# A chunked DeltaNet mixer: decay tiles E in a ring of three, keys scaled on VectorE, z and o loaded into the memory of the gated output

## The chip, the cores and the metric

The kernel runs on one core of a Trainium2 chip. The metric is the time of one execution on the device in microseconds (us), lower is better. TensorE is written PE (PEld for its weight loads), VectorE DVE, ScalarE ACT, GpSimd POOL and the engine that issues most loads SP. Each engine takes its instructions strictly in the order of the program; where an instruction waits, all behind it on that engine wait too. A DMA that SP issues waits in the same way in SP's order.

## The reference

The model is two layers over 512 latent tokens and 256 context tokens of width 1024. The change lies almost wholly in the mixer of the second, odd layer, a bidirectional chunked gated DeltaNet with 8 heads of width 128:

```python
q, k, v, a, b, z = project(h)            # h @ w_in; k, q, v through a 7-tap convolution and silu
k = l2norm(k); q = l2norm(q) * Dh ** -0.5
for dirn in (0, 1):                      # forward and backward
    g, beta = gates(a, b, dirn)
    # per chunk: gcum = cumsum(g)
    decay = exp(where(lower, gcum_i - gcum_j, -inf))
    lmat  = where(strict, (beta k) k^T * decay, 0)
    u, w  = triangular_solve(lmat, [beta v, beta k exp(gcum)])
    aqk   = where(lower, q k^T * decay, 0)
    # scan over chunks: state S, output o from q, S, aqk and u - w S
o = o * rsqrt(mean(o * o) + eps) * norm_g
out = (o * silu(z)) @ w_out
```

After the mixer come a SwiGLU half and the final norm.

## The kernel before

The whole kernel is written as Python generators, one for each strand of work (`conv`, `norms`, `pre`, `subst`, `loop`, `place`, `levels`, `scan`, `finish`, and the main strand). A planner (`Flow`) runs them: it keeps a clock for each engine, prices each instruction (`account`), and always resumes the strand that could start first. The program's order on each engine is the order in which the planner resumed them; on the chip nothing of it is decided again. A changed price therefore can move any instruction of the program, in both layers.

In the odd mixer, called `mixer1`, the chunk is 128 tokens (6 chunks, 4 of latent tokens). The main strand runs the 24 projections of k, q and v and then the 8 of z on PE; each result is copied to a `pad` tile by ACT and convolved by DVE. For each head, in order:

- `norms` transposes k to `kn`, sums squares on ACT, takes a reciprocal root in nine small DVE steps (`rsq_r`), and multiplies `kn` by it. That multiplication is on POOL. PE then transposes `kn` back into `kT`.
- `pre` loads the cumulative gates of the head as `E` (one tile for each direction, 384 KB from the DRAM tensor `gd`, by SP), masks it with one `affine_select` on POOL, exponentiates it in six ACT instructions, and multiplies the products of PE by it on DVE: first `NT` (from k with k), then `aq` (from k with q). `EB = 1`: there is one tile for each direction, so the two loads for the next head are issued when both `aq` of this head are done.
- `subst` and `loop` solve the 32 x 32 triangles: 31 steps of two POOL instructions (`s5l<-lm,xm` and `xm<-xm,s5l`), 62 for each head. `place` and `levels` put the blocks together (`fX`, `fP`, `fQ`) on DVE, PE and ACT.
- `scan` runs the chunks of the two directions (`u`, `O`); `finish` normalises `O`, transposes it and stores it to DRAM (`ogd`).

The projections of z go to DRAM too (`zd`). After the last of them the memory of the mixer's input is free: the residual `xT` (2 MB) is loaded back, and the output pair `oT` (`oTh`, `oTl`, a high and a low part) is allocated. The strand `gated` takes the heads one after the other: it loads z and o of a head into two work tiles, multiplies on DVE, rounds to `oTh` on ACT and takes the rest to `oTl` on DVE. The output projection (`gout`) follows: 8 groups of 18 matmuls over heads 0 to 5, and a last part over heads 6 and 7.

All instructions are recorded at one line, L207 (L208 after), so groups are told apart by their tiles.

Of the kernel before, what the change touches and what calls it, by code (L numbers as in the profile page):

```python
# [10 lines left out]
F32 = mybir.dt.float32  # L11
# [3 lines left out]
AF = mybir.ActivationFunctionType  # L15
# [3 lines left out]
P = 128  # L19
# [42 lines left out]
EB = 1  # L62
# [6 lines left out]
MP = 5000.0  # L69
MPS = 9000.0  # L70
LAG = 1000.0
CU = 2
UNITS = {"ffn02": 3, "ffn11": 4, "ffn12": 6}
WCH = ((19, 20), tuple(range(9)), tuple(range(9, 16)), (16, 17, 18, 21))
# [4 lines left out]
class Flow:  # L79
# [51 lines left out]
    def account(self, eng, op, a, k):  # L131
        self.used = self.used or eng
        aps = [v for v in (*a, *k.values()) if isinstance(v, bass.AP)]
        outs = [aps[0]] + ([k["accum_out"]] if k.get("accum_out") is not None else [])
        ins = [v for v in aps[1:] if v is not k.get("accum_out")]
        t = max(self.free[eng], *(self.ready(v, eng) for v in aps))
        n = 1
        for s in aps[0].shape[1:]:
            n *= s
        if op == "dma_start":  # L140
            b = 4.0
            for s in aps[0].shape:
                b *= s
            if eng == "gpsimd":
                self.free[eng] = t + 1040.0
                t += 1040.0
            else:
                self.free[eng] = t + 60.0
                t += 1100.0
            self.dma = max(self.dma, t) + b / 360.0  # L150
            self.sent = self.dma + 900.0
            self.note(aps[0], self.sent, "dma")
            return
        banks = [self.bank_of[v.tensor.name] for v in aps if v.tensor.name in self.bank_of]
        if eng == "tensor":
            c = max(n / 2.4 * (1 if ins[-1].dtype == F32R else 2 if op == "transpose" else 4), 27.0)
        elif eng == "scalar":
            c = n / 1.2 + (51.0 if ins[0].tensor.name in self.bank_of else 93.0)
            c += 93.0 * (len(outs) > 1 or isinstance(k.get("scale"), bass.AP) or isinstance(k.get("bias"), bass.AP))
            s = self.TABLE.get(k.get("func", a[2] if len(a) > 2 else None))  # L160
            self.uset = self.uset or s
            if s and s != self.table:
                self.table = s
                c += 1283.0
        elif eng == "vector":
            m = 1
            for s in ins[0].shape[1:] if ins else ():
                m *= s
            two = op in ("tensor_tensor", "tensor_add", "tensor_sub", "tensor_mul", "tensor_max")
            c = max(n, m) / 0.96 + (69.0 if two or len(ins) < 2 else 130.0)  # L170
            if op == "scalar_tensor_tensor" and not isinstance(a[2] if len(a) > 2 else k.get("scalar"), bass.AP):
                c -= 61.0
            if op in ("tensor_scalar", "tensor_copy") and not banks:
                c -= n / 1.92
        else:
            c = n * 0.83 + 140.0 if op == "affine_select" else n / 1.2 + 60.0 if op == "memset" else n * 2.05 + 145.0
        t += c
        self.free[eng] = t
        for v in outs:
            self.note(v, t, eng)  # L180
        for b in banks:
            self.bank_used[b] = max(self.bank_used[b], t)
        if t > self.end:
            self.end, self.last = t, eng
# [101 lines left out]
class Kern:  # L286
# [1622 lines left out]
    def mixer1(self, ph, nxt):  # L1909
        nc, A, tc, flow = self.nc, self.A, self.tc, self.flow  # L1910
        V = nc.vector
# [101 lines left out]
        def ht(name, shape, bufs=1, dt=F32):  # L2013
            return hpool.tile(shape, dt, name=name, tag=name, bufs=bufs)
# [63 lines left out]
        def norms():  # L2078

            yield ("gates",)  # L2080
            for hd in range(8):
# [7 lines left out]
                kn = R["kn"] = ht("kn", [P, 6, P], 3)  # L2089
# [19 lines left out]
                yield  # L2109
                V.tensor_scalar(sq, sq, EPS, None, op0=ALU.add)  # L2110
                rs = yield from self.rsqrt(self.small, sq, [P, 10], "h")
                nc.gpsimd.tensor_mul(kn, kn, rs[:, :6][:, :, None].to_broadcast([P, 6, P]))
                sg = R["sg"] = ht("sg", [P, 4], 3)
                V.tensor_scalar(sg, rs[:, 6:10], float(P) ** -0.5, None, op0=ALU.mult)
                sG = R["sG"] = ht("sG", [P, 2, 4], 3)
# [12 lines left out]
        def pre():  # L2128

            yield ("gates",)  # L2130
            def load(hd):

                E = [ht(f"E{d}", [P, 6, P], EB) for d in range(2)]
                for d in range(2):
                    nc.sync.dma_start(E[d].rearrange("p c i -> p (c i)"),
                                      bass.AP(tensor=gd.tensor, offset=gd.offset + (8 * d + hd) * 6 * P,
                                              ap=[[96 * P, 4], [0, 32], [1, 6 * P]]))
                return E

            yield ("gd",)  # L2140
            E1 = load(0)
            for hd in range(8):
                R = H[hd]

                E = E1 if EB == 2 or hd == 0 else load(hd)
                if EB == 2 and hd < 7:
                    E1 = load(hd + 1)
                for d in range(2):
                    yield flow.landed(E[d])
                    nc.gpsimd.affine_select(out=E[d], in_=E[d], pattern=[[0, 6], [1 - 2 * d, P]], base=0,  # L2150
                                            channel_multiplier=2 * d - 1, compare_op=ALU.is_ge, fill=-1e30)
                    yield
                    for c in range(6):
                        nc.scalar.activation(E[d][:, c], E[d][:, c], AF.Exp, bias=nG[:, d, hd, c:c + 1])
                    yield flow.free_at("scalar")
# [25 lines left out]
                yield  # L2181
                for d in range(2):
                    V.tensor_mul(Q[d], pt.rearrange("p (c i) -> p c i", c=4), E[d][:, 0:4])
                    yield flow.free_at("vector")
                self.rel(pt)
                flow.set("aq", hd)
# [244 lines left out]
        def finish():  # L2431
            for hd in range(8):
# [15 lines left out]
                on = O.rearrange("p c i -> p (c i)")  # L2448
                nc.scalar.activation(on, pt, AF.Copy, scale=self.vecs[:, V_GNG:V_GNG + 1])
                self.rel(pt)  # L2450
                nc.sync.dma_start(ogd[hd], on)
                flow.set("finish", hd)

        for n, g, p in (("conv", conv(0), 4), ("conv", conv(1), 4), ("norms", norms(), 3), ("pre", pre(), 3), ("values", values(), 2), ("blocks", subst(), 2), ("subst", loop(), 2), ("place", place(), 2), ("levels", levels(), 2), ("scan0", scan(0, 0), 1),
# [26 lines left out]
        op = ops.enter_context(tc.tile_pool(name="oT", bufs=1))  # L2481
        oT = (op.tile([P, 8, NX], F32R, name="oTh"), op.tile([P, 8, NX], F32R, name="oTl"))

        def gated():
            for hd in range(8):
                z, o = (self.work.tile([P, 512], F32, name=f"{n}{hd}", tag="sq0", bufs=2) for n in ("zg", "og"))
                nc.sync.dma_start(z, zd[hd])
                if ("finish", hd) not in flow.flags:
                    yield ("finish", hd)
                nc.sync.dma_start(o, ogd[hd])  # L2490
                yield max(flow.landed(o), flow.landed(z))
                V.tensor_mul(o, o, z)
                nc.scalar.activation(oT[0][:, hd], o, AF.Copy)
                V.tensor_sub(oT[1][:, hd], o, oT[0].bitcast(F32)[:, hd])
                flow.set("oT", hd)
                yield

        flow.spawn(gated(), name="gated", prio=2)

        for j in range(8):  # L2500
            a = (yield from self.get())
# [305 lines left out]
```

## Time and profile before

| | us |
|---|---|
| median of 3 runs | 2976.41 (2975.65 to 2981.3) |
| the profiled execution, its own time | 2976.59 |
| span of its instructions | 2974.8 |
| odd mixer, last projections of z stored | about 2477 |
| odd mixer, last part of `gout` starts | about 2570 |

Times in views count from the first instruction. In the groups "busy" is the time in which an engine worked, and the idle time is put down to what ended it. The granted clock is that of PE, 1.00 being 2.4 GHz and 0.50 being 1.2 GHz.

### The profile page before, as it was taken

The numbers are of one execution on the slowest core, as the hardware profiler recorded it, in microseconds if no ns is written. First come the engines' busy times: TensorE is split into PE (matmuls) and PEld (weight loads), VectorE is DVE, ScalarE is ACT, GpSimd is POOL, SyncE is SP. The second block draws the span as 40 slices with busy tenths as digits, with TensorE's granted clock in tenths as the row PEclk, the third lists the DMA queues.
The fourth block names the chain that finished last, engine by engine and source line by source line (L and its number), as shares of the span: only waits on it lengthen the run. The fifth ranks groups of instructions, "written<-read, shape, count | busy, mean of one in ns | idle before, by whom it ended". The sixth has DMA issues, their size and how long they took to land.

```text
span 2974.8 us, 47032 instructions
## 1 busy us (share of the span) xinstructions
PE 2772.8 (93%) x18380; PEld 2520.1 (85%) x18380; DVE 2053.5 (69%) x3941; ACT 1241.7 (42%) x2464; POOL 703.8 (24%) x1210
## 2 busy tenths in 40 slices
PE   7999999999999999999899999997878988889998
PEld 3888888898888999988899998896767877789977
DVE  6898863366728788743879985357676876688844
ACT  3221221234336444422544442246566765455532
POOL 1334341031311100000210111041755384100011
PEclk9999999999999999999999999998989999899999
DMA  6555432213512544442154665222101123224441
GB/s 234 171 169 181 165 112 82 64 61 93 122 46 85 174 160 147 167 131 80 42 205 161 231 228 181 79 77 84 54 33 54 39 94 115 102 83 132 140 157 57
DMA packets 99247, 356.41 MB, mean 120 GB/s; under 512 B 12448, under 2 KB 16192, under 8 KB 97360
## 3 DMA queue, kind: packets, MB, share of 16 engines
q1 hardware_dynamic: 57552, 192.12, 19.6%
q0 software_dynamic: 38144, 157.09, 16.0%
q10 hardware_dynamic: 3328, 4.20, 0.5%
q8 instruction: 144, 2.36, 0.3%
q14 instruction: 79, 0.65, 0.1%
HBM read 308.10 MB, written 45.25 MB: 119 GB/s over the span
## 4 chain that ended last, share of the span: by engine, by line
PE 68%; DVE 11%; POOL 7%; issue 5%; DMA 5%; ACT 3%; DVEq 0%; POOLq 0%; SPq 0%; ACTq 0%
PE ps L207 68%; POOL xm L207 2%; POOL s5l L207 2%; DVE mscr L207 1%; DMA E<-gd 1%; DVE wlo L207 1%; POOL z L207 1%; DMA grffn<-gdffn 1%; DMA wf<-in_wmodf_dram 1%; DVE xT L207 1%; DVE nt L207 1%; DVE rsq_a L207 1%; DVE h7l L207 1%; DMA z<-in_s5c_dram 1%; ACT whi L207 1%
## 5 line engine op out<-in xcount | busy, mean ns | idle before, releaser
L207 ACT ACTIVATE whi<-raw 128x1024 fp32r<-128x1024 f32 (+1 forms) x324 | 315.9, 978 | 646.2 <-PE ps L207 638.0
L207 DVE TENSOR_TENSOR wlo<-raw,whi 128x1024 fp32r<-128x1024 f32 (+1 forms) x310 | 351.3, 1134 | 337.8 <-ACT whi L207 337.2
L207 PE MATMUL ps<-hhi,whi 128*128 128x256 f32 (+1 forms) x1304 | 456.4, 350 | 0.5 <-ACT gg L207 0.5
L207 PE MATMUL ps<-hlo,whi 128*128 128x256 f32 (+1 forms) x1304 | 440.7, 338 | 1.1 <-DVE hlo L207 1.1
L207 PE MATMUL ps<-hhi,wlo 128*128 128x256 f32 (+1 forms) x1304 | 439.3, 337 | 2.0 <-DVE wlo L207 1.4
L207 PE MATMUL ps<-h7h,whi 128*128 128x256 f32 (+1 forms) x976 | 298.9, 314 | 4.1 <-ACT whi L207 4.0
L207 PE MATMUL ps<-h7h,wlo 128*128 128x256 f32 (+1 forms) x976 | 297.1, 312 | 4.8 <-DVE wlo L207 4.7
L207 PE MATMUL ps<-ghffn,whi 128*128 128x256 f32 (+1 forms) x896 | 297.6, 332 | 2.9 <-ACT whi L207 2.5
L207 PE MATMUL ps<-h7h,sh 128*128 128x384 f32 (+1 forms) x960 | 293.4, 318 | 6.9 <-ACT cffn L207 6.8
L207 PE MATMUL ps<-ghffn,wlo 128*128 128x256 f32 (+1 forms) x896 | 296.2, 331 | 2.9 <-DVE wlo L207 2.9
L207 PE MATMUL ps<-glffn,whi 128*128 128x256 f32 (+1 forms) x896 | 297.2, 332 | 0.7 <-DVE glffn L207 0.7
L207 PE MATMUL ps<-h7h,sl 128*128 128x384 f32 (+1 forms) x960 | 293.2, 317 | 3.5 <-DVE sl L207 3.5
L207 DVE SCALAR_TENSOR_TENSOR xT<-ps,gate,xT 128x256 f32<-128x256 f32 (+1 forms) x352 | 194.6, 576 | 129.8 <-PE ps L207 128.8
L207 PEld LDWEIGHTS ps<-hhi,wlo 128*128 128x128 f32 x1304 | 250.8, 192 | 31.2 <-DVE wlo L207 1.8
L207 PEld LDWEIGHTS ps<-hhi,whi 128*128 128x128 f32 x1304 | 251.4, 193 | 26.9 <-issue 1.2
L207 PEld LDWEIGHTS ps<-hlo,whi 128*128 128x128 f32 x1304 | 251.8, 193 | 25.1 <-DVE hlo L207 1.9
L207 PE MATMUL ps<-h7l,whi 128*128 128x256 f32 (+1 forms) x976 | 217.9, 313 | 1.9 <-DVE h7l L207 1.9
L207 ACT ACTIVATE cffn<-ps 128x384 f32<-128x384 f32 (+1 forms) x300 | 131.6, 450 | 197.6 <-PE ps L207 196.4
L207 POOL TENSOR_TENSOR sqsum<-sqsum,sq 128x256 f32<-128x256 f32 x96 | 78.2, 815 | 523.7 <-ACT sq L207 439.6
L207 PEld LDWEIGHTS ps<-h7h,wlo 128*128 128x128 f32 x976 | 188.2, 193 | 5.6 <-DVE wlo L207 5.6
L207 PEld LDWEIGHTS ps<-h7h,whi 128*128 128x128 f32 x976 | 188.1, 193 | 5.0 <-ACT whi L207 4.4
L207 PEld LDWEIGHTS ps<-h7h,sh 128*128 128x128 f32 x960 | 181.5, 189 | 7.6 <-ACT cffn L207 7.3
(350 smaller groups left out, 6372.4 us busy)
## 6 DMA issues: line engine op xcount, KB each, us to landing
raw<-in_ffn_dram SPq DMA_DIRECT2D x264, 512.0 KB
xT<-in_wmod_dram POOLq DMA_DIRECT2D x72, 512.0 KB, 4.7
wm<-in_wmod_dram POOLq DMA_DIRECT2D x56, 512.0 KB, 3.9
raw<-in_gin_dram SPq DMA_DIRECT2D x33, 512.0 KB
grffn<-gdffn POOLq DMA_DIRECT2D x40, 384.0 KB, 4.3
gdffn<-cffn POOLq DMA_DIRECT2D x36, 384.0 KB, 2.6
wf<-in_wmodf_dram POOLq DMA_DIRECT2D x16, 512.0 KB, 8.0
xd<-xT POOLq DMA_DIRECT2D x2, 3072.0 KB, 11.0
```

Source lines behind the costliest of these rows:

```text
L207: r = f(*a, **k)
```

## The change

`E` becomes one ring of three tiles for both directions, and a strand of its own issues the loads: load number n = 2 x head + direction waits for the `aq` of number n - 3. So direction 0 of the next head is loaded while this head is worked on, and direction 1 when `aq` of direction 0 of this head is done. The multiplication of `kn` moves from POOL to DVE. At the end, z is loaded by two DMAs of 1 MB straight into `oTh`, o of heads 0 to 5 into `oTl`, six strands gate them, and heads 6 and 7 (`LATE = 6`) are gated from `O` in SBUF with no store and load. The planner's prices change in two places: a load into a tile whose name begins with E lands 4500 ns after its transfer (900 before), and a POOL arithmetic instruction of n elements costs 2.1 n + 300 ns (2.05 n + 145 before).

```diff
+LATE = 6
...
-            self.sent = self.dma + 900.0
+            self.sent = self.dma + (900.0 if aps[0].tensor.name[:1] != "E" else 4500.0)
...
-            c = n * 0.83 + 140.0 if op == "affine_select" else n / 1.2 + 60.0 if op == "memset" else n * 2.05 + 145.0
+            c = n * 0.83 + 140.0 if op == "affine_select" else n / 1.2 + 60.0 if op == "memset" else n * 2.1 + 300.0
...
-                nc.gpsimd.tensor_mul(kn, kn, rs[:, :6][:, :, None].to_broadcast([P, 6, P]))
+                V.tensor_mul(kn, kn, rs[:, :6][:, :, None].to_broadcast([P, 6, P]))
...
-                E = [ht(f"E{d}", [P, 6, P], EB) for d in range(2)]
                 for d in range(2):
-                    nc.sync.dma_start(E[d].rearrange("p c i -> p (c i)"),
+                    if 2 * hd + d >= 3:
+                        yield ("E", 2 * hd + d - 3)
+                    t = ht("E", [P, 6, P], 3)
+                    nc.sync.dma_start(t.rearrange("p c i -> p (c i)"),
...
+                    Es[hd, d] = t
+                    flow.set("El", hd, d)
...
+            flow.spawn(loads(), name="loadE", prio=1)
             for hd in range(8):
                 R = H[hd]
-                E = E1 if EB == 2 or hd == 0 else load(hd)
-                if EB == 2 and hd < 7:
-                    E1 = load(hd + 1)
+                E = []
                 for d in range(2):
+                    if ("El", hd, d) not in flow.flags:
+                        yield ("El", hd, d)
+                    E.append(Es[hd, d])
...
                     V.tensor_mul(Q[d], pt.rearrange("p (c i) -> p c i", c=4), E[d][:, 0:4])
+                    flow.set("E", 2 * hd + d)
...
-                nc.sync.dma_start(ogd[hd], on)
+                if hd < LATE:
+                    nc.sync.dma_start(ogd[hd], on)
+                else:
+                    yield ("zg",)
+                    gate(hd, on)
...
-        def gated():
-            for hd in range(8):
-                z, o = (self.work.tile([P, 512], F32, name=f"{n}{hd}", tag="sq0", bufs=2) for n in ("zg", "og"))
-                nc.sync.dma_start(z, zd[hd])
-                if ("finish", hd) not in flow.flags:
-                    yield ("finish", hd)
-                nc.sync.dma_start(o, ogd[hd])
-                yield max(flow.landed(o), flow.landed(z))
-                V.tensor_mul(o, o, z)
-                nc.scalar.activation(oT[0][:, hd], o, AF.Copy)
-                V.tensor_sub(oT[1][:, hd], o, oT[0].bitcast(F32)[:, hd])
-                flow.set("oT", hd)
-                yield
+        of = [t.bitcast(F32) for t in oT]
...
+        def gate(hd, o):
+            p = self.work.tile([P, 512], F32, name=f"og{hd}", tag="sq0", bufs=2)
+            V.tensor_mul(p, o, of[0][:, hd])
+            nc.scalar.activation(oT[0][:, hd], p, AF.Copy)
+            V.tensor_sub(oT[1][:, hd], p, of[0][:, hd])
+            flow.set("oT", hd)
+
+        def gated(hd):
+            if ("finish", hd) not in flow.flags:
+                yield ("finish", hd)
+            nc.sync.dma_start(of[1][:, hd], ogd[hd])
+            yield flow.ready(of[1][:, hd], "vector") + 1500.0
+            if ("zg",) not in flow.flags:
+                yield ("zg",)
+            gate(hd, of[1][:, hd])
+
+        for i in range(2):
+            nc.sync.dma_start(of[0][:, 4 * i:4 * i + 4], zd[4 * i:4 * i + 4].rearrange("h p n -> p h n"))
+        flow.flags["zg",] = flow.ready(of[0], "vector")
+        for hd in range(LATE):
+            flow.spawn(gated(hd), name="gated", prio=2)
```

On POOL, from the first mask of head 0 to the masks of head 1, the program before has the scaling of `kn` after head 0's masks and starts the first loop between the two masks of head 1 (`s5l<-lm,xm` and `xm<-xm,s5l` are that loop):

```order
L207 AFFINE_SELECT E_18716<-E_18716 128x768
L207 AFFINE_SELECT E_18717<-E_18717 128x768
L207 MEMSET pad 128x3 x3
L207 TENSOR_TENSOR kn<-kn,rsq_r 128x768
L207 MEMSET pad 128x3 x3
L207 AFFINE_SELECT E_19010<-E_19010 128x768
L207 TENSOR_TENSOR s5l_78<-lm,xm 128x31
L207 TENSOR_TENSOR xm<-xm,s5l_78 128x31
...
L207 AFFINE_SELECT E_19011<-E_19011 128x768
```

In the changed program the same stretch of POOL reads:

```order
L208 AFFINE_SELECT E<-E 128x768 x2
L208 MEMSET pad 128x3 x6
L208 AFFINE_SELECT E<-E 128x768
L208 TENSOR_TENSOR s5l_78<-lm,xm 128x31
L208 TENSOR_TENSOR xm<-xm,s5l_78 128x31
...
L208 AFFINE_SELECT E<-E 128x768
```

The scaling has left POOL; four instructions of the loop stand between the masks of head 1 in both programs. Later heads' masks stand in the middle of the loop of the head before, after 10 to 36 of its 62 instructions.

On PE, behind the products k with q of head 0, the program before has at once the four transposes of q of head 1, which need that q to be convolved and through silu on ACT; the projections (`hhi`, `hlo` with `whi`, `wlo`) wait behind them:

```order
L207 MATMUL ps_18986<-qT,kT 128x128 x4
L207 MATMUL ps_19049<-ident,qT 128x128 x4
L207 MATMUL ps_19054<-hhi,whi_18794 128x512
L207 MATMUL ps_19054<-hlo,whi_18794 128x512
L207 MATMUL ps_19054<-hhi,wlo_18795 128x512
```

In the changed program projections come first there:

```order
L208 MATMUL ps_18987<-qT,kT 128x128 x4
L208 MATMUL ps_19048<-hhi,whi_18780 128x512
L208 MATMUL ps_19048<-hlo,whi_18780 128x512
...
L208 MATMUL ps_19147<-hhi,wlo_18905 128x256
L208 MATMUL ps_19170<-ident,qT 128x128 x4
```

The transposes of q have moved behind 90 matmuls of the projections.

On SP, behind the last store of z, the program before loads z and o of a head in turn, with a wait for DVE between the heads:

```order
L207 DMA zd<-z 128x512
L207 DMA xT_23283<-xspill 128x4096
L207 DMA zg_23291<-zd 128x512
L207 DMA og_23292<-ogd 128x512
L207 DMA raw_23311<-in_gout_dram 128x1024
L207 DMA zg_23450<-zd 128x512
```

In the changed program all of z is asked for at once, and o of heads 0 to 4 right behind it:

```order
L208 DMA xT<-xspill 128x4096
L208 DMA oTh<-zd 128x4x512 x2
L208 DMA oTl<-ogd 128x512 x5
L208 DMA raw_23229<-in_gout_dram 128x1024
L208 DMA ogd<-O 128x512
L208 DMA oTl<-ogd 128x512
```

The last two rows are head 5's. Between the loads of z and o of heads 0 to 4 nothing waits for DVE any more; o of head 0 now stands behind 4 MB of `xT` and z instead of behind 2.25 MB.

## Rows read from the trace of the kernel before

**Rows 1.** The page: busy us, share of the span, instructions.

```profile
PE 2772.8 (93%) x18380; PEld 2520.1 (85%) x18380; DVE 2053.5 (69%) x3941; ACT 1241.7 (42%) x2464; POOL 703.8 (24%) x1210
```

**Rows 2.** Stretches: length, busy us of PE, PEld, DVE, ACT, POOL; clock; DMA.

```profile
0.00:700.00 700.00, 663.73 (x4172) 558.80 (x4172) 466.28 (x978) 187.31 (x319) 196.21 (x256) 0.99 0.43 137
2000.00:2480.00 480.00, 397.85 (x3236) 347.93 (x3235) 336.82 (x703) 317.59 (x868) 273.83 (x592) 0.91 0.18 62
2480.00:2519.00 39.00, 29.60 (x304) 25.02 (x304) 25.55 (x75) 19.43 (x61) 9.14 (x25) 0.96 0.41 144
2519.00:2563.00 44.00, 42.77 (x229) 35.98 (x230) 26.70 (x74) 17.09 (x52) 0.00 (x0) 0.96 0.25 78
```

**Rows 3.** The chain that ended last, 2000 to 2571 us, its shares by line.

```profile
by line: PE ps L207 37.3%; POOL xm L207 11.9%; POOL s5l L207 11.6%; issue 7.8%; DMA E<-gd 6.9%; DMA og<-ogd 2.3%; POOL E L207 2.0%; DVE kT L207 2.0%; POOL kn L207 1.6%; DVE wlo L207 1.3%; DMA ogd<-O 1.1%; DVE NT L207 1.1%; DVE aq L207 1.0%;
```

**Rows 4.** Waits, 2000 to 2571 us: us in total, times, longest.

```profile
POOL E L207 <- DMA E<-gd: 59.5, 9, 21.7
POOL kn L207 <- DVE rsq_r L207: 21.5, 3, 10.3
...
PE ps L207 <- POOL kn L207: 20.6, 5, 8.2
PE ps L207 <- ACT qT L207: 16.7, 1, 16.7
PE ps L207 <- DVE u L207: 16.3, 6, 8.0
```

**Rows 5.** Timeline at head 1's masks: start, us, engine, instruction, idle time before it.

```profile
2065.54 1.16 SPq L207 DMA_DIRECT2D E<-gd  x2
...
2073.44 0.86 POOL L207 TENSOR_SCALAR_AFFINE_SELECT E<-E 128x768 f32<-128x768 f32 x1 [21.65 <-DMA E<-gd]
...
2073.35 1.28 ACT L207 ACT_TABLE_LOAD   x1 [7.42 <-DMA E<-gd]
...
2078.50 1.11 PE L207 MATMUL ps<-ident,qT 128*128 128x128 f32 x4 [16.73 <-ACT qT L207]
```

**Rows 6.** Timeline at head 1's scaling of the keys.

```profile
2094.11 0.40 DVE L207 SCALAR_TENSOR_TENSOR rsq_r<-rsq_a,rsq_r 128x10 f32<-128x10 f32 x1
...
2104.37 1.47 POOL L207 TENSOR_TENSOR kn<-kn,rsq_r 128x768 f32<-128x768 f32 x1
...
2105.89 1.12 PE L207 MATMUL ps<-ident,kn 128*128 128x128 f32 x4 [8.20 <-POOL kn L207]
```

**Rows 7.** Groups, 2000 to 2600 us: busy us, mean ns, idle before.

```profile
L207 POOL TENSOR_TENSOR kn<-kn,rsq_r 128x768 f32<-128x768 f32 x8 | 12.6, 1579 | 21.5 <-DVE rsq_r L207 21.5
...
L207 DVE TENSOR_TENSOR O<-O,rsq_r 128x512 f32<-128x512 f32 x8 | 5.7, 717 | 0.2
```

**Rows 8.** The stretch just after PE's longest wait, columns as above.

```profile
2078.00:2082.00 4.00, 3.50 (x11) 2.92 (x12) 2.10 (x3) 3.90 (x13) 3.53 (x11) 0.50 0.00 0
```

**Rows 9.** The chain and PE's timeline where head 7 is gated.

```profile
2563.91 2.00 DMA ogd<-O
...
2565.93 2.68 DMA og<-ogd
...
2570.04 0.58 PE L207 MATMUL ps<-oTh,whi 128*128 128x256 f32 x1 [5.18 <-ACT oTh L207]
```

**Rows 10.** PE's timeline inside a projection.

```profile
2058.42 0.40 PE L207 MATMUL ps<-hhi,wlo 128*128 128x512 f32 x1
2058.66 0.39 PE L207 MATMUL ps<-hhi,whi 128*128 128x512 f32 x1
```

**Rows 11.** The stretch in which `xT`, z and o of head 0 land; the last column is GB/s.

```profile
2476.00:2488.00 12.00, 10.53 (x92) 9.37 (x90) 8.45 (x26) 9.07 (x33) 10.05 (x25) 1.00 0.76 286
```

**Rows 12.** PE's waits in the first 700 us.

```profile
PE ps L207 <- DVE z L207: 6.1, 4, 2.6
PE ps L207 <- POOL z L207: 4.6, 3, 2.4
```

More of the change, by code (lines that the diff above doesn't have):

```diff
@@ L2131, in load, with loads @@
             def load(hd):
-                E = [ht(f"E{d}", [P, 6, P], EB) for d in range(2)]
                 for d in range(2):
-                    nc.sync.dma_start(E[d].rearrange("p c i -> p (c i)"),
+                    if 2 * hd + d >= 3:
+                        yield ("E", 2 * hd + d - 3)
+                    t = ht("E", [P, 6, P], 3)
+                    nc.sync.dma_start(t.rearrange("p c i -> p (c i)"),
                                       bass.AP(tensor=gd.tensor, offset=gd.offset + (8 * d + hd) * 6 * P,
                                               ap=[[96 * P, 4], [0, 32], [1, 6 * P]]))
-                return E
-            yield ("gd",)
-            E1 = load(0)
+                    Es[hd, d] = t
+                    flow.set("El", hd, d)
+            Es = {}
+            def loads():
+                yield ("gd",)
+                for hd in range(8):
+                    yield from load(hd)
+            flow.spawn(loads(), name="loadE", prio=1)
             for hd in range(8):
                 R = H[hd]
-                E = E1 if EB == 2 or hd == 0 else load(hd)
-                if EB == 2 and hd < 7:
-                    E1 = load(hd + 1)
+                E = []
                 for d in range(2):
+                    if ("El", hd, d) not in flow.flags:
+                        yield ("El", hd, d)
+                    E.append(Es[hd, d])
                     yield flow.landed(E[d])
@@ L2482, in mixer1 @@
         oT = (op.tile([P, 8, NX], F32R, name="oTh"), op.tile([P, 8, NX], F32R, name="oTl"))
-        def gated():
-            for hd in range(8):
-                z, o = (self.work.tile([P, 512], F32, name=f"{n}{hd}", tag="sq0", bufs=2) for n in ("zg", "og"))
-                nc.sync.dma_start(z, zd[hd])
-                if ("finish", hd) not in flow.flags:
-                    yield ("finish", hd)
-                nc.sync.dma_start(o, ogd[hd])
-                yield max(flow.landed(o), flow.landed(z))
-                V.tensor_mul(o, o, z)
-                nc.scalar.activation(oT[0][:, hd], o, AF.Copy)
-                V.tensor_sub(oT[1][:, hd], o, oT[0].bitcast(F32)[:, hd])
-                flow.set("oT", hd)
-                yield
-        flow.spawn(gated(), name="gated", prio=2)
+        of = [t.bitcast(F32) for t in oT]
[18 more added lines that the diff above has]
+            flow.spawn(gated(hd), name="gated", prio=2)
         for j in range(8):
```

## The prediction

> **What bounds the kernel now.** I read the page's engine line first, then the stretches, the chain, the waits, and the timeline at the places where the waits are long. PE is the busiest engine, 93% of the span [rows 1], so a saving outside PE counts only where it shortens PE's idle time. The stretches say where that is: in the first 700 us PE idles 700 - 663.7 = 36.3 us, but in the odd mixer from 2000 to 2480 us it idles 480 - 397.9 = 82.1 us, and its granted clock is 0.91 there, so part of the work ran at 1.2 GHz instead of 2.4 [rows 2]. DVE is busy 70% of that stretch and POOL 57%: neither is full, and what binds is the order in which the three wait for each other. From 2480 to 2519 us PE idles another 9.4 us, and from 2519 to 2563 us only 1.2 us [rows 2].
>
> The chain from 2000 to 2571 us runs through PE for 37% and through the POOL loop for 23.5%; 6.9% of 571 us, 39.4 us, are loads of E that it waits for, and 1.6% is the scaling of `kn` on POOL [rows 3]. The waits name the same things: POOL waits 59.5 us for E in nine places, and PE waits 20.6 us for `kn` on POOL and 16.7 us, in one piece, for q of head 1 on ACT [rows 4].
>
> That one piece shows how a load stops three engines. The two loads of E for head 1 are issued at 2065.54, the mask on POOL starts at 2073.44 after 21.65 us of idleness, ACT stands 7.42 us before the exponentials of E, and behind them in ACT's order is the silu of q that PE's transposes need: PE starts again at 2078.50, 16.73 us late [rows 5].
>
> **The change, part by part.** All sums are made against the profiled execution, 2976.6 us; the median of the runs shown is 0.2 us below it.
>
> *The ring of E.* Direction 0 of a head is loaded one head early, so its mask, and the exponentials that stand in front of other ACT work, no longer wait. Direction 1 is still issued late, when `aq` of direction 0 of the head before is done, and the load of head 1 shows 2073.44 - 2065.54 = 7.9 us from issue to use [rows 5]; but the planner now knows that and puts its mask further back. What PE has of it: at head 1 the transposes of q stand behind 90 projection matmuls instead of none. Such matmuls start 0.24 us apart [rows 10], so there are 21 us of other work over a wait of 16.7. The gain there is between 0 (the projections stall on banks or on the copies to `pad`, which ACT does behind the same exponentials) and 16.7. I take 12. The first wait of POOL, for head 0, stays: nothing is ahead of it. The other E waits on the chain, 39.4 - 16.7 = 22.7 us at most, fall on POOL while PE has projections to do; I count nothing for them and keep 22.7 for the low end.
>
> *The scaling on DVE.* At head 1 the reciprocal root is ready at 2094.11 + 0.40 = 2094.51, but POOL gets to `kn` at 2104.37, behind its loop, and PE waits 8.20 us for it [rows 6]. On DVE the multiplication stands right behind the root. The 20.6 us of PE's waits [rows 4] are thus mostly POOL's queue; where POOL itself waited for the root (21.5 us, three places [rows 4]) nothing is won. What is added on DVE: the nearest instruction, `O` by a broadcast root, takes 717 ns for 512 elements [rows 7]; in proportion 768 elements take 1.08 us, against 1.58 us on POOL [rows 7]. Eight of them are 8.6 us on an engine with 480 - 336.8 = 143 us idle in that stretch [rows 2], so they are hidden except the one that PE waits for. If DVE's idle time were gone they would cost 8.6. I take 14 of the 20.6, with bounds 6 and 19.
>
> By the Trainium skill's page "SBUF — State Buffer", section "Who interferes with whom", a DVE instruction with two inputs in SBUF holds the read port that POOL also uses, so that a POOL instruction that reads SBUF stops for it. By that rule the eight multiplications would stop POOL's loop for up to 8.6 us, and the move would free 12.6 - 8.6 = 4 us of POOL, not 12.6. Since the sum counts PE's waits and not POOL's time, it would stay as it is; the rule makes a gain on POOL alone doubtful. No row of before has this multiplication on DVE, so the trace can't weigh the rule here.
>
> *The clock.* After PE's long wait the clock is 0.50 from 2078 to 2082 us, and that stretch did 3.5 us of work at half rate [rows 8], about 2 us lost. There are two more waits for `kn` of some length within the 20.6 us, so I give back 2 us once and 1 us each for the two, 4; bounds 0 and 6.
>
> *Gating heads 6 and 7 in place.* The chain at the end is the store of o, 2.00 us, and its load, 2.68 us, and PE waits 5.18 us there [rows 9]. Both DMAs go; the multiply, the rounding and the rest stay. That is 4.7 us of path with nothing beside it, since PE has finished all that it could do. I take 4.7 (bounds 4 and 5.2). For head 6 the same round trip lies in a stretch where PE is busy 42.8 of 44 us [rows 2]: nothing.
>
> *z and o into the output's memory.* o of head 0 now comes behind 2.1 MB of `xT` and 2.1 MB of z. The rate was 286 GB/s there [rows 11], so that is 4.5 MB, 16 us, where it was 2.6 MB, 9 us: the first head is gated some 7 us later, but the next five at once and not one after the other. PE's idle time from 2480 to 2519 is 9.4 us [rows 2] and could go or double. I take 0, bounds -9 and +9.
>
> *The order elsewhere.* The new price of POOL arithmetic moves S5 work of layer 0 by up to 33 rows of PE's order. PE waits there for `z` 6.1 + 4.6 us in all [rows 12]; I take 0, with 5 either way.
>
> Sum: 12 + 14 + 4 + 4.7 = 34.7, so 2976.6 - 34.7 = **2942 us**.
>
> **The rivals.** *(A) E was the chain.* All E waits on the chain and all of PE's waits for `kn` turn into time: 39.4 + 19 + 6 + 4.7 = 69, 2908 us. For it: POOL's loop and E together are a third of the chain [rows 3]. Against it: scan waits, such as PE for `u`, 16.3 us [rows 4], have another cause and stay.
>
> *(B) The waits change their names.* The third tile helps direction 0 only; direction 1 is issued as late as before, and the scan steps, which PE waits for today, stop it sooner. Then a quarter of the two PE waits (37.3 / 4 = 9) and the end, 4.7, remain: 2963 us. For it: of PE's 82 us of idle time in the mixer E and `kn` own only 37. Against it: the transposes of q have left the place where PE stood longest.
>
> *(C) Slower: projections overtake head 7.* The higher POOL price makes the planner put the products for head 7's `NT` behind 1254 of the 1272 projection matmuls, before behind 1218, and its first `levels` step behind 57 `gout` matmuls, before behind 9. At 0.24 us each [rows 10] head 7 starts 36 x 0.24 = 8.6 us later against the end of the projections, and 48 x 0.24 = 11.5 us later against the start of `gout`: 20 us on the path that ends last. It decides if the projections end less than 20 us earlier by the first terms. With what (B) saves, 13.7, the result is 2976.6 + 20 - 13.7 = 2983 us. Against it: those matmuls have to be done anyhow, and from 2519 us on PE was almost full [rows 2].
>
> *(D) It is hidden anyway*: PE's projections bound the mixer, and only small pieces remain, within 0.2%, about 6 us, which is what a measurement of this kernel can tell from no change.
>
> **How the numbers follow.** My forecast (2925 to 2955) has 0.50, (A) 0.17, (B) 0.19, (C) 0.09, (D) 0.05. Faster by over 0.2% is the first three, 0.86; within it, (D), 0.05; slower, (C), 0.09. The range must leave out no more than 0.2: I reach to (A) with 2908 and to a little past (B) with 2968, and leave (C) and (D) and the far side of (A) out.
>
> **What would show it.** In the profile after, POOL's waits for E should be near 21 us (head 0) plus small pieces for direction 1; PE's wait for q of head 1 and those for `kn` should be gone or below 5 us in all; `kn` should stand on DVE with about 1.1 us each; the clock of the mixer should be above 0.91; the stretch before the last part of `gout` should show no DMA between `O` and the gating. Waits for `u`, `O` and `NT` on PE that grow by as much as those vanish would be (B); PE idle between the last projection and head 7's `levels` would be (C). I would be wrong in the first place if the new strand's direction 1 loads come so late that POOL and ACT stand as before.

## The result and the profile after

The changed kernel takes 2948.0 us (median of 4 runs, 2944.41 to 2950.42), the kernel before 2978.86 (4 runs, 2975.65 to 2983.89): ratio 0.9895, with a 95% interval of 0.9881 to 0.9909. That is 31 us faster; 34.7 had been forecast. The profiled execution took 2946.45 us, 30.1 less than that of before, and the rows below are its rows. Of run a8 below, one execution of 8084.74 us is left out of median and ratio; its other five took 2955.56 to 2966.34 us.

First the page's line of engines, as in [rows 1], and the stretches of [rows 2] with the same columns:

```profile
PE 2767.9 (94%) x18380; PEld 2510.5 (85%) x18380; DVE 2068.9 (70%) x3949; ACT 1248.7 (42%) x2468; POOL 715.4 (24%) x1202
```

```profile
0.00:700.00 700.00, 661.43 (x4090) 556.15 (x4090) 456.94 (x967) 185.07 (x315) 192.11 (x253) 0.99 0.42 136
2000.00:2480.00 480.00, 420.47 (x3421) 363.98 (x3420) 381.45 (x779) 340.52 (x920) 298.88 (x612) 0.96 0.22 75
2480.00:2519.00 39.00, 38.61 (x353) 32.79 (x352) 25.11 (x66) 20.51 (x58) 0.00 (x0) 1.00 0.17 55
2519.00:2563.00 44.00, 29.57 (x196) 26.89 (x195) 29.56 (x70) 16.28 (x41) 13.39 (x14) 0.85 0.21 71
```

PE's busy time is the same to 5 us. From 2000 to 2480 us its idle time is 480 - 420.5 = 59.5 us, where it was 82.1 [rows 2], with a clock of 0.96 for 0.91; from 2480 to 2519 it is 0.4, where it was 9.4. But these stretches are cut by the clock, and the changed kernel is some 30 us further on in the last two; the last one holds the end of the mixer and the start of the half behind it. Cut by the work, the mixer has two parts: from the store of `gd`, which opens the heads, to the last matmul of the projections, and from there to the last `oTl`. Before, then after, with the columns of [rows 2]:

```profile
2032.40:2472.80 440.40, 360.75 (x2978) 315.83 (x2978) 311.58 (x656) 293.43 (x826) 257.91 (x556) 0.91 0.18 60
2472.80:2570.70 97.90, 81.59 (x619) 68.64 (x617) 59.07 (x160) 44.48 (x130) 15.36 (x38) 0.95 0.34 114
```

```profile
2043.30:2441.10 397.80, 350.85 (x2868) 303.07 (x2867) 321.40 (x651) 293.94 (x817) 257.10 (x519) 0.95 0.20 66
2441.10:2542.00 100.90, 82.87 (x727) 70.04 (x726) 68.28 (x172) 49.52 (x143) 29.68 (x66) 0.95 0.29 101
```

The first part is 42.6 us shorter, and PE's idle time in it falls from 79.7 to 47.0 us. The second part, where the edits of the gating lie, is 3.0 us longer. So the first part carries more than the whole gain, and some 11 us are lost again ahead of it, where the store of `gd` comes later.

The chain's shares by line from 2000 to 2571 us, against [rows 3], and the waits there (us in total, times, longest), against [rows 4]; after the change this window holds 29 us of the half behind the mixer:

```profile
by line: PE ps L208 47.3%; DVE kT L208 5.5%; DVE sqsum L208 4.8%; issue 3.6%; DVE rsq_a L208 3.5%; DVE wlo L208 3.1%; ACT modv L208 3.0%; DVE rsq_r L208 2.8%; DVE O L208 2.1%; DVE NT L208 2.0%; DVE u L208 1.7%; DMA E<-gd 1.5%; ACT whi L208 
```

```profile
POOL E L208 <- DMA E<-gd: 21.7, 4, 14.3
...
PE ps L208 <- DVE O L208: 18.2, 13, 5.4
...
PE ps L208 <- DVE kn L208: 13.6, 4, 10.6
...
PE ps L208 <- ACT u L208: 9.1, 8, 3.1
...
PE ps L208 <- DVE u L208: 7.6, 9, 3.4
...
PE ps L208 <- ACT qT L208: 2.5, 1, 2.5
```

POOL's loop, 23.5% of the chain before, is gone from these leading shares. E on the chain fell from 6.9% to 1.5%, POOL's waits for E from 59.5 us to 21.7, and PE's wait for q from 16.7 to 2.5. In the loop's place stand DVE's convolution (`kT`) and its short steps (`rsq_a`, `rsq_r`). PE's wait for `kn` did not go: it has DVE as its cause now, 13.6 us where POOL was the cause of 20.6.

The longest of these, at head 1, is in the timeline of DVE and PE (start, us, engine, instruction, idle time before it); it answers to [rows 6]:

```profile
2094.35 0.41 DVE L208 TENSOR_SCALAR sqs<-sqs 128x10 f32<-128x10 f32 x1
...
2094.87 1.22 DVE L208 SCALAR_TENSOR_TENSOR kT<-pad,vecs,kT 128x771 f32<-128x771 f32 x1
2096.01 1.45 DVE L208 TENSOR_TENSOR wlo<-raw,whi 128x1024 fp32r<-128x1024 f32 x1
2097.39 0.39 DVE L208 TENSOR_SCALAR rsq_r<-rsq_r 128x10 int32<-128x10 int32 x1
...
2107.06 0.40 DVE L208 SCALAR_TENSOR_TENSOR rsq_r<-rsq_a,rsq_r 128x10 f32<-128x10 f32 x1
2107.50 0.96 DVE L208 TENSOR_TENSOR kn<-kn,rsq_r 128x768 f32<-128x768 f32 x1
...
2108.51 1.12 PE L208 MATMUL ps<-ident,kn 128*128 128x128 f32 x4 [10.61 <-DVE kn L208]
```

`kn` does stand right behind the root, 0.04 us after it. But the twelve small steps that lead to it (three ahead of the nine of the root), mostly 0.4 us each, stand between convolution steps and `wlo` of 0.7 to 1.45 us, so that the root takes 2107.46 - 2094.35 = 13.1 us. Before, the same twelve steps stood between the same kinds of instructions and took 2094.51 - 2081.85 = 12.7 us; their end is in [rows 6], their start is

```profile
2081.85 0.29 DVE L207 TENSOR_SCALAR sqs<-sqs 128x10 f32<-128x10 f32 x1
```

Counted from the store of `gd` (2032.4 us before, 2043.3 after), the root ends after 62.1 us before and 64.2 after. PE is ready for `kn` after 65.3 and 54.6 us, and gets it after 73.5 and 65.2. So `kn` comes 8.3 us sooner, but PE comes 10.7 us sooner, and it now waits for the root.

The groups from 2000 to 2600 us (busy us, mean ns, idle before), which answer to [rows 7]; the first two are POOL's loop:

```profile
L208 POOL TENSOR_TENSOR xm<-xm,s5l 128x126 f32<-128x126 f32 (+22 forms) x248 | 133.3, 538 | 19.4
L208 POOL TENSOR_TENSOR s5l<-lm,xm 128x126 f32<-128x126 f32 (+22 forms) x248 | 132.8, 535 | 97.4 <-DVE lm L208 33.0 <-issue 20.1 <-DVE u L208 18.8
...
L208 DVE TENSOR_TENSOR kn<-kn,rsq_r 128x768 f32<-128x768 f32 x8 | 7.9, 988 | 0.3
```

And the chain at the end of the mixer, where head 7 is gated, against [rows 9]:

```profile
2500.01 32.05 PE ps L208 x223
...
2537.25 0.70 DVE O L208
2538.00 1.13 PE ps L208 x4
2539.20 0.70 ACT O L208
2539.92 0.70 DVE og L208
2540.65 0.64 ACT oTh L208
2541.31 0.70 DVE oTl L208
2542.06 3.14 PE ps L208 x13
```

No DMA stands between `O` and the last part of `gout`; before there were two, 2.00 and 2.68 us.

### The profile page after: what moved, and what is told of

It reads as the page before. It is cut to its first block, busy times and chain, and to the rows that moved or that the text cites. A ratio compares the mean times of both kernels' runs of the same rounds, so it can differ in the third digit from the quotient of the medians.

```text
span 2944.7 us, 47007 instructions
## 1 busy us (share of the span) xinstructions
PE 2767.9 (94%) x18380; PEld 2510.5 (85%) x18380; DVE 2068.9 (70%) x3949; ACT 1248.7 (42%) x2468; POOL 715.4 (24%) x1202
## 4 chain that ended last, share of the span: by engine, by line
PE 71%; DVE 14%; issue 4%; ACT 4%; DMA 4%; POOL 3%; DVEq 0%; POOLq 0%; SPq 0%; ACTq 0%
PE ps L208 71%; DVE wlo L208 1%; POOL z L208 1%; DVE rsq_a L208 1%; DVE kT L208 1%; DVE mscr L208 1%; DVE sqsum L208 1%; DMA grffn<-gdffn 1%; DMA wf<-in_wmodf_dram 1%; DVE rsq_r L208 1%; DMA z<-in_s5c_dram 1%; DMA wm<-in_wmod_dram 1%; DVE nt L208 1%; DVE xT L208 1%; ACT whi L208 1%
## 5 line engine op out<-in xcount | busy, mean ns | idle before, releaser
L208 PEld LDWEIGHTS ps<-hhi,whi 128*128 128x128 f32 x1304 | 249.5, 191 | 26.8 <-issue 1.0
## 6 DMA issues: line engine op xcount, KB each, us to landing
xd<-xT POOLq DMA_DIRECT2D x2, 3072.0 KB, 11.6
```

What stands on the lines that cost most here:

```text
L208: r = f(*a, **k)
```

## The experiments

Each ratio is to the kernel before, timed beside the program. The gain is (1 - ratio) x 2978 us, about the median of before; an interval of a ratio is some 4 to 5 us to either side, so a difference of two gains is known to about 6 us.

| run | median us | ratio (95%) | gain, us |
|---|---|---|---|
| the change | 2948.0 | 0.9895 (0.9881 to 0.9909) | 31.3 |
| a1 POOL price new in the odd mixer alone | 2940.84 | 0.9875 (0.9862 to 0.9889) | 37.2 |
| a2 before, with both new prices | 2997.81 | 1.0064 (1.0051 to 1.0077) | -19.1 |
| a3 `kn` back on POOL | 2953.46 | 0.9918 (0.9905 to 0.9932) | 24.4 |
| a4 ring of two tiles | 2961.49 | 0.9947 (0.9934 to 0.9961) | 15.8 |
| a5 all heads stored and loaded | 2953.59 | 0.9913 (0.9900 to 0.9926) | 25.9 |
| a6 the gating of before | 2964.7 | 0.9954 (0.9941 to 0.9967) | 13.7 |
| a7 price of E as before | 2956.2 | 0.9923 (0.9911 to 0.9935) | 22.9 |
| a8 POOL price as before | 2956.07 | 0.9934 (0.9917 to 0.9951) | 19.7 |
| b1 both prices as before | 2961.75 | 0.9940 (0.9925 to 0.9956) | 17.9 |
| b2 a1 with `LATE = 5` | 2948.25 | 0.9893 (0.9875 to 0.9911) | 31.9 |
| b3 before, with `kn` on DVE alone | 2996.39 | 1.0061 (1.0046 to 1.0077) | -18.2 |
| b4 a1 with E priced at 6500 | 2950.77 | 0.9910 (0.9894 to 0.9927) | 26.8 |

**The ring (a4).** Two tiles in place of three; the rest of the change stays.

```diff
-                    if 2 * hd + d >= 3:
-                        yield ("E", 2 * hd + d - 3)
-                    t = ht("E", [P, 6, P], 3)
+                    if 2 * hd + d >= 2:
+                        yield ("E", 2 * hd + d - 2)
+                    t = ht("E", [P, 6, P], 2)
```

> The changed kernel with two tiles E in the ring instead of three, so that each load waits for the aq of its own direction of the head before, as before the change. My theory: POOL's waits for E go from 21.7 us back to 40 to 60, and the time is 2958 to 2972 us. Rival: the loads are hidden by the order that the planner makes for a late E; POOL's waits for E stay under 30 us and the time is 2944 to 2952.

It lost 31.3 - 15.8 = 15.5 us. The waits of a4 and its chain, 2000 to 2571 us:

```profile
POOL E L208 <- DMA E<-gd: 79.1, 8, 23.6
...
ACT L208 <- DMA E<-gd: 15.1, 2, 7.9
```

```profile
by line: PE ps L208 37.2%; POOL s5l L208 8.6%; POOL xm L208 8.1%; issue 7.7%; DMA E<-gd 7.0%; DVE kT L208 2.4%; POOL E L208 2.3%; DVE wlo L208 2.0%; ACT whi L208 1.6%; DVE lm L208 1.6%; ACT E L208 1.5%; ACT modv L208 1.5%; DVE rsq_r L208 1.
```

Everything that [rows 3] and [rows 4] show of E is back: POOL waits for it eight times, ACT stands with it, and 7.0% of the chain are its loads. With the rest of the change in place, the third tile takes 79.1 - 21.7 = 57.4 us of POOL's waits away. The planner's prices move these waits too: they are 37.1 us with three tiles and the old price of E (a7), and 38.3 in the kernel before with the new prices (a2), where [rows 4] has 59.5.

**The scaling (a3 and b3).** In a3 `kn` goes back to POOL in the changed kernel; in b3 it goes to DVE in the kernel before, and nothing else changes.

```diff
-                V.tensor_mul(kn, kn, rs[:, :6][:, :, None].to_broadcast([P, 6, P]))
+                nc.gpsimd.tensor_mul(kn, kn, rs[:, :6][:, :, None].to_broadcast([P, 6, P]))
```

> The changed kernel with the scaling of the keys back on POOL. My theory: PE's waits for kn come back in part (20.6 us before, 13.6 us in the changed kernel, of which the most is one wait of 10.6), and the time is 2956 to 2964 us. Rival: kn was never the limit, since PE waits for the reciprocal root anyway and VectorE has become the chain; then 2944 to 2951.

> The kernel before with the scaling of the keys on VectorE and nothing else. The prediction put 14 us on this part; undone in the changed kernel it cost 5 to 6. My theory: alone it gains 4 to 14, since PE's waits for kn on POOL (20.6 us) shrink but those for the reciprocal root stay: 2965 to 2975 us. Rival: PE's waits simply go to POOL's waits for E, and it is the same as before; 2975 to 2982.

a3 lost 6.9 us, less than the theory's 8 to 16 and little more than the comparison can tell. b3 was neither faster nor nearly unchanged, as the two sides had it, but 18.2 us slower. Groups of a3, then of b3, 2000 to 2600 us:

```profile
L208 POOL TENSOR_TENSOR xm<-xm,s5l 128x126 f32<-128x126 f32 (+22 forms) x248 | 130.2, 525 | 19.4
L208 POOL TENSOR_TENSOR s5l<-lm,xm 128x126 f32<-128x126 f32 (+22 forms) x248 | 123.2, 497 | 80.3 <-ACT NT L208 19.4 <-DVE lm L208 17.2 <-DVE O L208 13.0
...
L208 POOL TENSOR_TENSOR kn<-kn,rsq_r 128x768 f32<-128x768 f32 x8 | 14.9, 1858 | 11.0 <-DVE rsq_r L208 8.1 <-ACT pad L208 2.9
```

```profile
L207 POOL TENSOR_TENSOR xm<-xm,s5l 128x126 f32<-128x126 f32 (+22 forms) x248 | 128.3, 517 | 19.4
L207 POOL TENSOR_TENSOR s5l<-lm,xm 128x126 f32<-128x126 f32 (+22 forms) x248 | 121.0, 488 | 136.2 <-ACT modv L207 33.3 <-DMA xm<-in_unitx_dram 31.3 <-DVE og L207 28.1
...
L207 DVE TENSOR_TENSOR kn<-kn,rsq_r 128x768 f32<-128x768 f32 x8 | 8.2, 1024 | 0.1
```

The instructions of b3's loop are not what makes it slow: they sum to 249.3 us, against 238.8 before and 266.1 in the change. POOL stands idle 136.2 us in front of its loop, against 63.9 before; 31.3 of that is put down to the load of `xm`, and 28.1 to the gating on DVE, just in front of head 7's loop. PE does lose its waits for `kn` in b3, but they are replaced by others: in its mixer PE waits 17.0 us for ACT's `sqsum` and 23.8 us for DVE's `u`. The planner has moved the heads in all three engines, and the last of the loop ends at 2529.4 us (2490.4 before). Cut by the work as above, b3's first part is 442.7 us, 2.3 longer than before, and its second 111.5, 13.6 longer: most of the loss lies behind the last projection. Which of the moved instructions costs it was not separated.

**The prices (a2, a7, a8, b1, a1, b4).** a2 is the kernel before with the two prices of the change; the others start from the change, where a7 takes the price of E back, a8 that of POOL, and b1 both. In a1 the new POOL price holds only once the odd mixer has begun, and b4 is a1 with 6500 in place of 4500 ns for E.

```diff
-            self.sent = self.dma + 900.0
+            self.sent = self.dma + (900.0 if aps[0].tensor.name[:1] != "E" else 4500.0)
...
-            c = n * 0.83 + 140.0 if op == "affine_select" else n / 1.2 + 60.0 if op == "memset" else n * 2.05 + 145.0
+            c = n * 0.83 + 140.0 if op == "affine_select" else n / 1.2 + 60.0 if op == "memset" else n * 2.1 + 300.0
```

The second of these lines in a1, with `flow.odd = True` at the head of `mixer1`:

```diff
-            c = n * 0.83 + 140.0 if op == "affine_select" else n / 1.2 + 60.0 if op == "memset" else n * 2.1 + 300.0
+            c = n * 0.83 + 140.0 if op == "affine_select" else n / 1.2 + 60.0 if op == "memset" else n * 2.1 + 300.0 if self.odd else n * 2.05 + 145.0
```

> The kernel before with nothing but the two new prices of the planner. My theory: the gain is from the third tile and from the scaling on VectorE, not from the prices; here the 7 us of layer 0 are lost, POOL's waits for E fall somewhat below 59.5 us since the masks stand further back, and the time is 2970 to 2986 us. Rival: the order that the new prices make is what gained; then 2945 to 2958.

> The changed kernel with the old price of a load into E (900 ns after its transfer, not 4500). My theory: the third tile does the work, but the masks of direction 1 stand too far ahead on POOL; POOL's waits for E go from 21.7 to 30 to 45 us and the time is 2950 to 2962. Rival: the ring alone hides the loads; 2944 to 2950.

> The changed kernel with the old price of POOL arithmetic throughout. The run in which the new price held only in the odd mixer took 2940.8 us, with the same planner up to the mixer. My theory: in the mixer the new price makes projections overtake head 7 (first levels step of head 7 behind 57 matmuls of the output projection, with the old price behind 36), so the old one is better: 2930 to 2939 us. Rival: POOL's loop is really slower than the old price says, and the new order fits it better; 2944 to 2956 us.

> The changed kernel with both prices of the planner as they were; ring, scaling on VectorE and gating stay. Undone alone, the late landing of E cost 8 us and the POOL price, kept out of layer 0 in the comparison, 17 us; the two prices alone on the kernel before cost 19 us. My theory: the parts and the prices belong together, the parts alone gain about half; 2955 to 2968 us. Rival: without the prices the parts gain little or nothing; 2970 to 2980.

> The changed kernel with the new POOL price used only once the odd mixer begins; before that the planner has the old price. My theory: the new price costs about 7 us in layer 0 (the store of the residual before the odd mixer is issued at 1982.8 instead of 1975.6 us) and buys nothing there, so the store is back at 1975.6 +- 1 and the time falls to 2937 to 2942 us, the best so far. Rival: the 7 us are not the price's doing, or come back later as waits in the odd mixer; then the time stays at 2945 to 2950.

> The best version so far with a load into E priced at 6500 ns after its transfer instead of 4500, nearer to the 7.9 us that the load of head 1 took before. My theory: masks go a little further back, POOL's waits for E after head 0 (7 us) shrink and the time is 2936 to 2942. Rival: masks that come late hold up the exponentials and the NT products; 2943 to 2952.

The prices alone made the kernel before 19.1 us slower, more than either side expected; 13.4 of it lie in the second part of the mixer (111.3 us for 97.9). Taken out of the change, each cost time: E's 31.3 - 22.9 = 8.4 us, POOL's 11.6, both 13.4. So the theory of a8, that the POOL price harms, fell; those of a7 and b1 came true. The chain of a8, 2000 to 2571 us:

```profile
by line: PE ps L208 37.5%; POOL xm L208 19.7%; POOL s5l L208 17.9%; issue 7.1%; DVE lm L208 1.6%; POOL E L208 1.6%; DVE NT L208 1.4%; DVE wlo L208 1.1%; DVE rsq_r L208 1.0%; DVE O L208 1.0%; ACT whi L208 0.9%; DVE rsq_a L208 0.9%; ACT E L20
```

The loop is 37.6% of it, though `kn` is gone from POOL and of the waits for E only that of head 0, 18.6 us, is left. My reading is that the loop, priced too low, was planned to end sooner than it does, and that what needs it was put too far ahead. The loop's instructions average 92 elements; the old price makes that 2.05 x 92 + 145 = 334 ns, the new one 493, and the trace has 535 to 538 after. The new price is nearer for this loop. That a nearer price takes the loop off the chain is not shown: b4, which has it too, has 19.1% of its chain there.

In front of the odd mixer the same price costs time. From the spill of `xT` to the store of `gd`, seven executions with the old price ahead of the mixer (before, a1, a8, b1 to b4) took 56.3 to 58.3 us, and seven with the new one 60.5 to 61.4: about 4 us. It is the price ahead of the mixer that counts here, since a1, b2 and b4 have the new one from just in front of the spill on. The 7 us that a1's theory put ahead of the spill are not there: the spill is issued at 1973.7 to 1982.0 us in the seven with the old price, which have the same order on PE up to it, and at 1977.6 to 1982.8 in the others, so the 1982.8 and 1975.6 that it compared lie within what executions differ by. a1, which has the new price only where the loop is, has the best ratio of all, and is 17.5 us faster than a8, which has it nowhere; in their traces 11.9 us of that lie in the first part of the mixer (400.9 and 412.8 us) and 5.3 in the second (101.1 and 106.4). Over the change its 5.9 us are as large as what the comparison can tell; 4 of them have this place. b4 shows that a higher price for E is no further gain: it lost 10.4 us against a1, and POOL's waits for E rose from 21.7 to 27.8 us instead of shrinking.

**The end of the mixer (a5, a6, b2).** In a5 heads 6 and 7 go through DRAM like the rest, but z and o still land in `oTh` and `oTl`. a6 has the strand `gated` of before, with its two work tiles, and all heads stored.

```diff
-LATE = 6
+LATE = 8
```

```diff
+        def gated():
+            for hd in range(8):
+                z, o = (self.work.tile([P, 512], F32, name=f"{n}{hd}", tag="sq0", bufs=2) for n in ("zg", "og"))
+                nc.sync.dma_start(z, zd[hd])
...
+                nc.sync.dma_start(o, ogd[hd])
...
-        for i in range(2):
-            nc.sync.dma_start(of[0][:, 4 * i:4 * i + 4], zd[4 * i:4 * i + 4].rearrange("h p n -> p h n"))
...
+        flow.spawn(gated(), name="gated", prio=2)
```

> The changed kernel with LATE = 8, so that o of heads 6 and 7 goes through DRAM again. My theory: the round trip of head 7 is back with nothing beside it, 4.7 us, and the time is 2950 to 2956 us. Rival: the end is not bound by it; 2945 to 2949.

> The changed kernel with the whole gating as before: z and o of each head through two work tiles, one head after the other, all heads through DRAM. My theory: head 7's round trip costs 4.7 us and the loads straight into the output's memory are worth nothing more, as predicted; 2950 to 2956 us. Rival: taking the heads one after the other starves PE, whose output projection now has 57 matmuls ahead of head 7; then 2957 to 2970.

> The best version so far (new POOL price in the odd mixer alone, 2940.8 us) with LATE = 5: head 5 is gated in place as well. My theory: head 5's round trip through DRAM stood between its finish and the sixth k of the first output group, where PE idles a little; 2935 to 2941. Rival: z is not there yet when head 5 is finished, or VectorE is in the way; 2941 to 2947.

a5 lost 5.4 us and a6 17.6, so the loading of z and o is worth 12.2 of these, which the prediction had at nothing. The 5.4 are within what the comparison can tell, but the traces place both: the first part of the mixer is 400.7 us in a5 and 400.8 in a6, and the second 106.8 and 119.6, for 100.9 in the change. In a6's timeline DVE stands still for the loads of the second to the fifth head (two of them here), and the waits from 2436 to 2570 us have PE behind it:

```profile
2458.95 0.69 DVE L208 TENSOR_TENSOR og<-og,zg 128x512 f32<-128x512 f32 x1 [1.35 <-DMA og<-ogd]
...
2463.86 0.69 DVE L208 TENSOR_TENSOR og<-og,zg 128x512 f32<-128x512 f32 x1 [2.31 <-DMA og<-ogd]
```

```profile
DVE og L208 <- DMA og<-ogd: 18.9, 6, 6.5
...
PE ps L208 <- ACT oTh L208: 13.3, 5, 6.1
```

a6 gates its first five heads from 2454.0 to 2475.5 us, one in 5.4 us, and the sixth, whose o is stored only at 2483.1, at 2490.6. The change gates the six from 2461.6 to 2474.2, one in 2.5. Its start is 7.6 us later, as the prediction said, and its end 16.4 earlier. PE's wait for `oTh` there is 2.4 us after and 13.3 in a6. b2, one head more gated in place, gains nothing over a1. Its loss of 5.3 us isn't shown to come from the gating: the two profiled executions lie 7.3 us apart, and 6.4 of that lie ahead of the store of `gd`, which this edit does not touch.

## Why the prediction came out as it did

The time lies 6 us above the forecast, in its own range. Two terms came about near their size, the ring and the gating of heads 6 and 7. The scaling was put too high, the loading of z and o too low, and the prices inside the mixer had no term.

*The ring of E*, put at 12: the undoing costs 15.5. POOL's waits for E are 21.7 us where it said near 21 and small pieces, but head 0 has only 14.3 of them. The transposes of q stand 2.5 us instead of 16.7.

*The scaling on DVE*, put at 14 of 20.6: the undoing costs 6.9, at the low bound. The step that failed is "the 20.6 us of PE's waits are thus mostly POOL's queue": it counted the wait from the root on, for a PE that comes when it came before. At head 1 the root took 12.7 us between convolution steps on DVE even then, and ended only 3.2 us before PE was ready. The change made PE ready 10.7 us sooner and the root no sooner, so PE waits 10.6 us there, 9.6 of them until the root is done. The waits for `kn` "gone or below 5 us in all" are 13.6. On DVE it takes 0.99 us, where 1.08 was estimated.

*POOL's time.* The rule that the prediction held beside its sum can be weighed now. From before to b3 the loop's 496 instructions take 249.3 - 238.8 = 10.5 us longer, and from a3 to the change 266.1 - 253.4 = 12.7, where `kn` lasts 8.2 and 7.9 us on DVE; POOL was freed of 12.6 and 14.9. These pairs don't weigh it, since the order differs in both: a2, with `kn` still on POOL, has the loop at 256.0 us, 17.2 above before. On DVE `kn` runs beside the loop for only 5.0 us in b3 and 6.7 in the change, so the move itself gave back no more than about that much. But the loop runs beside other DVE instructions with two inputs in SBUF, and the prediction was wrong that the trace of before can't weigh the rule:

```profile
2393.24 0.74 DVE L207 SCALAR_TENSOR_TENSOR qT<-pad,vecs,qT 128x512 f32<-128x512 f32 x1
2393.37 0.91 POOL L207 TENSOR_TENSOR s5l<-lm,xm 128x126 f32<-128x126 f32 x1
...
2394.23 0.59 DVE L207 SCALAR_TENSOR_TENSOR O<-ps,sg,O 128x128 f32<-128x128 f32 x2
2394.36 0.45 POOL L207 TENSOR_TENSOR xm<-xm,s5l 128x126 f32<-128x126 f32 x1
```

Both POOL instructions have 126 elements. The first runs beside a DVE instruction that reads two tensors from SBUF (`pad` and `qT`), the second beside one that has one of its two in PSUM (`ps`). Of the loop's 48 instructions of this size, those beside no DVE instruction of the first kind take 431 to 437 ns in the mean in each of the fourteen programs (before, after and the twelve runs), and those beside one 696 to 929 ns. The Trainium skill's page "SBUF — State Buffer", section "Who interferes with whom", has DVE and POOL share one pair of ports, with an exclusive lock; the trace agrees that they get in each other's way just there, but that the lock is exclusive isn't shown.

*The clock*, put at 4: from 2000 to 2480 us it rose from 0.91 to 0.96 as said. From the store of `gd` to the last `oTl`, PE did as many matmuls (3597 and 3595) in 442.3 us of busy time before and 433.7 after; if the clock is all of that, it is worth 8.6 us. No run separates it.

*Gating heads 6 and 7 in place*, put at 4.7: the undoing costs 5.4, its trace has the second part of the mixer 5.9 us longer, and the two DMAs are gone from the chain.

*z and o into the output's memory*, put at 0 with 9 either way: 12.2, outside the bound by less than the 6 us of the comparison. The step named both sides, the first head later and the next five at once, and then took them as equal. It also measured them by PE's idle time of before, 9.4 us from 2480 to 2519 [rows 2]. In the changed mixer the projections end 42.6 us sooner, and a6 shows what the old loading would cost there: PE idles 28.5 us in the second part, against 16.3 before and 18.0 after.

*The order elsewhere*, put at 0 with 5 either way: the entrance of the mixer costs 4 us, inside that bound. The prices inside the mixer had no term of gain at all; there the POOL price is worth 17.5 us and E's 8.4.

*The rivals.* (C) had the order right and its cost wrong. Before, the first `levels` step of head 7 comes 29.9 us behind the last projection, after the change 50.2: 20.3 us later against the projections, as its sum had it. PE is idle for 6.0 and 10.5 us of these stretches. It asked that the projections end less than 20 us earlier, and they end 42.6 us earlier, counted from the store of `gd`. The last `oTl` comes only 3.0 us later against them. With the old gating the second part grows wherever head 7's loop starts behind the last projection (111.3 us in a2, 111.5 in b3, 119.6 in a6, for 97.9 before). So the new gating seems to have paid for what (C) feared; no run separates that. The POOL price is not to blame: with the old one (a8) the second part is 106.4 us and the first 412.8. (B) came true for `kn` alone, where 13.6 of 20.6 us changed their name; PE's waits for `u`, `O` and `NT`, which should have grown, fell from 44.9 us to 39.9 in all. (A) needed all of E off the chain and all of PE's waits for `kn` gone; 1.5% and 13.6 us of them stayed. (D) is out.

The undoings don't add up: 15.5 + 6.9 + 5.4 + 12.2 for the four edits and 13.4 for the prices are 53.4, against 31.3 for all. From the other side, the edits without the prices (b1) gain 17.9 and the prices without the edits (a2) lose 19.1. Each program has an order of its own, so an undoing also moves instructions that it isn't about. A price that is nearer seems to pay only together with the edits; why is not shown. That the prediction's total was close is in part luck: z, o and the prices were missing on one side, the scaling was too large on the other, and the parts overlap.

## What to carry to other kernels

Where a planner writes the order, cost its table of prices as an edit of its own: compare the price with the mean of the group that it prices, in the stretch where that engine is on the chain, and don't expect a part tried alone to show what it is worth in company. When a wait moves to an engine with idle time, look at what stands between the steps that feed it there, since an engine that is 70% busy can still take 13 us for twelve steps of 0.4, and ask whether the engine that waits will still come when it came before. Loads that wait for a small work tile, one pair after the other, are best counted by the pace that they set (5.4 us a head against 2.5), not by the first one's landing. And cut two traces by the work before comparing them, since equal times hold different work once one program is ahead.

## What was not expected of the hardware

The multiplication of `kn` takes 988 ns on DVE and 1579 (before) to 1858 ns (a3) on POOL for the same 128 x 768 elements. How long POOL's own instruction takes depends on what DVE does beside it. In each of the fourteen programs, the loop's instructions that ran beside no DVE instruction with two inputs in SBUF lie near one line, about 1.92 ns an element and 188 ns, which is 365 ns at the loop's mean of 92 elements. All 496 at that price would be 181 us, an estimate from these rows. The loop took 238.8 us before, when 154 of the 496 had such a neighbour, and 266.1 after, when 230 had. So the mean of POOL's loop went from 478 to 535 ns for `s5l` and from 485 to 538 for `xm`, with the same counts and sizes. A duration on POOL read from one program is therefore not that of the next, and the planner's new price, 493 ns at 92 elements, has DVE's part in it.
